# Layer 0 of a two-layer diffusion trunk: fewer gathered rows traced beside each expert product worked out ahead

## The chip, the cores and the metric

One Trainium2 chip, one of its cores. The metric is device time in microseconds (us) of one execution, lower is better. Times of different runs of the kernel before: 5150.38, 5170.73 and 5175.75 us, median 5170.73 us.

## The reference, cut to what matters

Two layers over 512 latent tokens and 256 context tokens, model width 1024. Each layer is a mixer and then PEER, an expert network with 128 x 128 = 16384 experts. For every token and each of 8 heads, 16 experts are retrieved, so 128 experts per token:

```python
    def block(xb):
        q = (xb @ w_q).reshape(P_TOKEN_BLOCK, P_HEADS, 2, P_DQ // 2)
        s = jnp.einsum('nhpd,hpkd->nhpk', q, keys).astype(jnp.float32)
        s_top, i_top = lax.top_k(s, P_TOPK)
        ...
        u = u_tab[idx]
        v = v_tab[idx]
        act = jax.nn.gelu(jnp.einsum('nd,nhkd->nhk', xb, u).astype(jnp.float32), approximate=False)
        return jnp.einsum('nhk,nhkd->nd', (gate * act).astype(v.dtype), v)
```

In layer 0 both streams need it: the 512 latent tokens and the 256 context tokens. The context result is read first by layer 1.

## The kernel before, in words

The kernel computes PEER in two ways. **Dense**, for the latent tokens of layer 0: all 16384 experts are multiplied with all 512 tokens, 128 experts (index j) at a time, and a gate table G that is zero for experts not chosen weighs the activations. **Sparse**, for the two tiles of 128 context tokens: `sparse` (L1710) gathers, one of 128 chosen experts after the other, a row of 1024 floats for each of the 128 tokens from the u table (indirect DMA issued by GpSimd, L1729), multiplies and sums it on VectorE (L1741); then the same from the v table, accumulated on VectorE (L1754). One such gather and its VectorE instruction is called a row here. Two tiles x 2 tables x 128 make 512 rows in layer 0.

The sparse work is a Python generator that yields after each row. `pull(n)` (L470) adds n to an account and takes one row out of the generator for each whole unit. Calls of `pull` stand at fixed places of the dense work, so they decide after which dense instruction a row is traced. `issue_after(s.anchor)` (L1728) holds each gather on GpSimd behind the last weight split (L354 or L233) that was traced before it. The row buffers `ga` are a ring: 4 in the first stage of layer 0 (`NS[0]`), 5 in the second (`NX` more), 7 in the second of layer 1. The tracing order is a priority: a planner (`schedule_with_timeline_sim`) lays out the order of each engine's instructions from it, and on the chip every engine keeps that order.

`peer(0)` (L1769) has two stages.

Stage one, the ahead stage. `retrieve` (L1567) makes 16 query products and scores, takes the top 16 on VectorE and decodes indices; `spread` (L1676) turns each tile's choice into one-hot matrices on VectorE and ScalarE (L1693, L1700, L1701, L1703), multiplies them on TensorE (L1705), collects 32 tokens in one staging buffer (`stg`, L1706) and writes it to the table G in DRAM. Between them, `u_step` (L1804) works out 96 of the 128 dense products activation(u_j . x) ahead of need (TensorE L250, L251, L253) and writes them to DRAM (AD). Query and u products both take 8 matmuls on each of those three lines. The generator of retrieve and spread yields a price; each 5.5 of it pays for a `u_step`, followed by a `pull`:

```python
                    if p == 0 and s.gens:
                        s.pull(2 * R0[l])
                    while price > UP[l] and n < spill:
                        price -= UP[l]
                        u_step()
                        n += 1
                        s.pull(R0[l])
                while n < spill:
                    u_step()
                    n += 1
                    s.pull(RT[l])
```

The yield with p == 0 comes 8 times (once per head). `UP[0]` is 5.5, `spill` 96, `RT[0]` 2. These lines are L1869 to L1879. The other prices: 3.6 per head for the top 16 of each of the three later token tiles (8 heads each), 2.6 four times per tile in the decoding of the indices, 1.2 thirty-two times per tile in `spread`; there are four tiles.

Stage two, the dense stage, `peer_out` (L1892). For each of 128 j: the activations (96 from AD, 32 worked out here) times G (L1932), split into high and low parts (ScalarE L230, GpSimd L233), the v rows likewise (L230, VectorE L233), then 18 matmuls into six accumulators (L1998 to L2000) and 6 more into a tile (L1916 to L1918) that VectorE adds to the result (L1920). A `pull(s.rate)` follows each j and each of the 32 products; `s.rate = s.left() / (128.0 + 128 - len(old)) + 0.02` (L1907) spreads what is left of the rows over these 160 places. `peer_out` starts only when all of G is written.

Layer 1 has the same two stages with other numbers (`R0[1]` = 1.6).

Of the kernel before, what the change touches and what calls it, by code (L numbers as in the profile page):

```python
# [27 lines left out]
GT = (0, 1)  # L28
HT = (0, 1)
PD = (1, 2)  # L30
R0 = (2.0, 1.6)
RG = (2, 1)
NR = 2
NV = 3
# [173 lines left out]
class Net:  # L208
# [1560 lines left out]
    def peer(s, l):  # L1769
# [11 lines left out]
        with ExitStack() as st:  # L1781
# [30 lines left out]
            with ExitStack() as es:  # L1812
# [53 lines left out]
                for p in s.chain([s.retrieve(l, ep, tp_, pk, (psq, 'q'), (psm, 'hs'), (hh, hl), tiles, max(ng + nh, 1),  # L1866
                                             done, after), halves()]):
                    price += p
# [8 lines that stand above are left out]
# [198 lines left out]
```

## Time and profile before

| | |
|---|---|
| median of 3 runs | 5170.73 us (5150.38 to 5175.75) |
| profiled execution, its own time | 5158.15 us |
| span of its trace | 5156.4 us |
| TensorE busy | 4427.5 us, 86% |
| VectorE busy | 3975.7 us, 77% |
| GpSimd busy | 2888.2 us, 56% |
| ScalarE busy | 2022.6 us, 39% |
| mean granted TensorE clock | 0.927 |

The profiled execution lies 12.58 us under the median of the runs and inside their spread. Busy shares are means over stages with different limits, so they are read stage by stage below. Windows are in us from the start of the span: in layer 0 the retrieval and the products ahead run from about 936 to 1872, the dense stage from 1872 to 2840; in layer 1 the dense stage runs from 4435 to 5122.

### The profile page before, as it was taken

How to read it: one execution, taken by the hardware profiler on the slowest of the kernel's cores; microseconds unless marked ns; L12 is line 12 of the kernel's file. 1: busy time of each engine (PE TensorE's matmuls, PEld its weight loads, DVE VectorE, ACT ScalarE, POOL GpSimd, SP SyncE). 2: the span in 40 equal slices, each digit the busy share in tenths (PEclk: the TensorE clock that was granted, in tenths of full speed). 3: DMA queues.
4: the chain of work that ended last, by engine and by line, in shares of the span. 5: the costliest groups of instructions: out<-in, count | busy, mean ns of one | idle time of the engine just before them, and what ended most of it. 6: DMA issues, size and time to landing. Idle time of an engine off the chain costs nothing. (4 is left out here: it accounts for less than half of the span.)

```text
span 5156.4 us, 74375 instructions
## 1 busy us (share of the span) xinstructions
PE 4427.5 (86%) x26350; PEld 3625.3 (70%) x26350; DVE 3975.7 (77%) x7777; ACT 2022.6 (39%) x3979; POOL 2888.2 (56%) x2244
## 2 busy tenths in 40 slices
PE   7899988788889979999999898897966677799897
PEld 5777667567778867777777675785765676677775
DVE  4665568899998868787878674662699989888896
ACT  3544442225555642222222365332333553233332
POOL 2342233776667846656665320542476686688884
PEclk8999998899999989999999997998988888899999
DMA  5432124677778988877787210004377787899995
GB/s 193 156 115 62 58 78 160 220 262 249 238 267 304 321 279 312 288 285 282 284 295 287 88 52 21 6 6 151 106 221 249 248 304 271 310 335 339 340 352 211
DMA packets 453558, 1109.55 MB, mean 215 GB/s; under 512 B 40640, under 2 KB 204864, under 8 KB 449088
## 3 DMA queue, kind: packets, MB, share of 16 engines
q1 hardware_dynamic: 323872, 633.91, 36.4%
q0 software_dynamic: 129312, 470.87, 25.5%
q8 instruction: 208, 3.41, 0.3%
q14 instruction: 166, 1.36, 0.1%
HBM read 995.58 MB, written 109.05 MB: 214 GB/s over the span
## 5 line engine op out<-in xcount | busy, mean ns | idle before, releaser
L354 POOL TENSOR_TENSOR wlo<-wraw,whi 128x512 fp32r<-128x512 f32 x810 | 1148.4, 1441 | 982.1 <-ACT whi L351 910.8
L1729 POOL DMA_INDIRECT ga<-in_pu,idx x512 | 672.5, 1313 | 361.8 <-DVE ga L1741 105.1
L253 PE MATMUL u<-hh,wlo 128*128 128x512 f32 (+1 forms) x2048 | 746.0, 365 | 103.1 <-POOL wlo L354 103.0
L1741 DVE SCALAR_TENSOR_TENSOR ga<-ga,htok 128x1024 f32<-128x1024 f32 x512 | 742.6, 1464 | 94.0 <-DMA ga<-in_pu,idx 93.6
L250 PE MATMUL u<-hh,whi 128*128 128x512 f32 (+1 forms) x2048 | 744.3, 363 | 51.7 <-DVE xl L1920 24.1
L251 PE MATMUL u<-hl,whi 128*128 128x512 f32 (+1 forms) x2048 | 734.6, 359 | 0.0
L351 ACT ACTIVATE whi<-wraw 128x1024 fp32r<-128x1024 f32 x405 | 426.2, 1054 | 748.4 <-PE u L251 361.0
L1754 DVE SCALAR_TENSOR_TENSOR sacc<-ga,sact,sacc 128x1024 f32<-128x1024 f32 x381 | 563.7, 1480 | 112.0 <-DMA ga<-in_pv,idx 107.4
L1729 POOL DMA_INDIRECT ga<-in_pv,idx x384 | 502.4, 1308 | 210.0 <-DVE sacc L1754 76.3
L253 PEld LDWEIGHTS u<-hh,wlo 128*128 128x128 f32 x2048 | 422.2, 206 | 154.2 <-POOL wlo L354 112.7
L250 PEld LDWEIGHTS u<-hh,whi 128*128 128x128 f32 x2048 | 423.5, 207 | 107.1 <-DVE xl L1920 33.4
L251 PEld LDWEIGHTS u<-hl,whi 128*128 128x128 f32 x2048 | 422.6, 206 | 40.9
L233 DVE TENSOR_TENSOR vl<-vraw,vh 128x768 fp32r<-128x768 f32 (+1 forms) x256 | 356.5, 1399 | 92.7 <-ACT vh L230 71.9
L1705 PE MATMUL g<-ohB,ohA 128*128 128x128 f32 x1792 | 300.4, 297 | 135.9 <-DVE ohB L1703 109.1
L1705 PEld LDWEIGHTS g<-ohB,ohA 128*128 128x128 f32 x1792 | 265.1, 204 | 182.6 <-DVE ohB L1703 100.9
L230 ACT ACTIVATE vh<-vraw 128x768 fp32r<-128x768 f32 (+1 forms) x256 | 240.0, 946 | 286.2 <-PE acc L1999 229.3
L1703 DVE TENSOR_SCALAR ohB<-c_all,pt 128x128 f32<-128x128 f32 x512 | 319.1, 648 | 40.4 <-PE g L1705 34.7
L2000 PE MATMUL acc<-wh,vl 128*128 128x512 f32 x768 | 302.8, 394 | 23.2 <-DVE vl L233 22.3
L1998 PE MATMUL acc<-wh,vh 128*128 128x512 f32 x768 | 290.0, 393 | 27.0 <-ACT wh L230 27.0
L1999 PE MATMUL acc<-wl,vh 128*128 128x512 f32 x768 | 301.1, 392 | 9.1 <-POOL wl L233 9.1
L2015 PE MATMUL acc<-vl,wh 128*128 128x512 f32 x768 | 258.3, 402 | 27.1 <-DVE vl L233 27.0
L2014 PE MATMUL acc<-vh,wh 128*128 128x512 f32 x768 | 222.1, 399 | 45.6 <-ACT vh L230 25.2
(514 smaller groups left out, 10063.8 us busy)
## 6 DMA issues: line engine op xcount, KB each, us to landing
wraw<-in_uT SPq DMA_DIRECT2D x256, 512.0 KB
vraw<-in_pv SPq DMA_DIRECT2D x256, 512.0 KB
G<-stg SPq DMA_DIRECT2D x28, 2048.0 KB
wraw<-in_ada_w SPq DMA_DIRECT2D x96, 512.0 KB
wraw<-in_ew SPq DMA_DIRECT2D x64, 512.0 KB
G<-G SPq DMA_DIRECT2D x32, 1024.0 KB
wraw<-in_pwq SPq DMA_DIRECT2D x48, 512.0 KB
AD<-act SPq DMA_DIRECT2D x96, 256.0 KB
```

Source lines behind the costliest of these rows:

```text
L233: i = (lo_eng or nc.vector).tensor_tensor(lo, x, hi.bitcast(F32), OP.subtract)
L250: nc.tensor.matmul(o, a, hh[:, k], start=(k == 0), stop=False)
L251: nc.tensor.matmul(o, a, hl[:, k], start=False, stop=False)
L253: nc.tensor.matmul(o, b, hh[:, k], start=False, stop=(k == nk - 1))
L351: nc.scalar.activation(hi[:, :, 0:m], r[:, :, 0:m], AF.Copy)
L354: i = nc.gpsimd.tensor_tensor(lo[:, p, 0:m], r[:, p, 0:m], hi[:, p, 0:m].bitcast(F32), OP.subtract)
L1703: nc.vector.tensor_scalar(B, C['iota'], pt[:, 1, c:c + 1], pt[:, 2, c:c + 1], op0=OP.is_equal, op1=OP.mult)
L1705: nc.tensor.matmul(ps[:, n], A[:, n], B, start=True, stop=True)
L1729: nc.gpsimd.indirect_dma_start(out=ga, out_offset=None, in_=tab, in_offset=bass.IndirectOffsetOnAxis(ap=idx[:, k:k + 1], axis=0))
L1741: nc.vector.scalar_tensor_tensor(ga, ga, 1.0, htok, op0=OP.mult, op1=OP.mult, accum_out=act[:, k:k + 1])
L1754: nc.vector.scalar_tensor_tensor(acc, ga, act[:, k:k + 1], acc, op0=OP.mult, op1=OP.add)
L2000: nc.tensor.matmul(acc[d], b, wh, start=False, stop=sp)
```

## The change

One constant. `R0[0]` goes from 2.0 to 1.2. It is read at two places, both shown above: `pull(2 * R0[l])` after each of the 8 heads of the retrieval, and `pull(R0[l])` after each product worked out ahead while the retrieval and the spreading are being traced. `RT`, the pull beside the products that are left after that, stays 2. Rows not pulled there remain in `s.left()`, and L1907 spreads them along the dense stage.

```diff
 PD = (1, 2)
-R0 = (2.0, 1.6)
+R0 = (1.2, 1.6)
 RG = (2, 1)
```

## Rows read from the trace of the kernel before

**Rows 1.** Windows, all engines: window, length, busy us (instructions) PE PEld DVE ACT POOL; clock, DMA share, GB/s
```profile
936.00:1100.00 164.00, 137.80 (x594) 109.62 (x595) 139.78 (x309) 47.98 (x106) 138.41 (x102) 0.90 0.79 260
1100.00:1485.00 385.00, 325.99 (x1510) 265.31 (x1509) 378.76 (x980) 182.14 (x363) 254.49 (x184) 0.93 0.75 253
1485.00:1600.00 115.00, 101.99 (x495) 84.17 (x494) 112.52 (x247) 62.49 (x133) 80.52 (x56) 0.94 0.77 259
1600.00:1830.00 230.00, 229.93 (x1205) 195.76 (x1205) 186.69 (x216) 142.93 (x313) 180.49 (x130) 1.00 0.90 315
1830.00:1872.00 42.00, 11.88 (x65) 10.24 (x63) 15.90 (x27) 18.96 (x45) 3.44 (x3) 0.64 0.65 226
1872.00:2840.00 968.00, 904.54 (x3789) 724.62 (x3790) 776.76 (x900) 264.54 (x441) 617.41 (x455) 0.97 0.82 292
4435.00:5122.00 687.00, 629.88 (x2957) 519.22 (x2958) 587.83 (x564) 224.92 (x312) 554.88 (x398) 0.97 0.93 334
```

**Rows 2.** Waits of PE, 1100 to 1600: total us, times, longest
```profile
PE g L1705 <- DVE ohB L1703: 46.1, 36, 3.6
```

**Rows 3.** Timeline of PE, 1830 to 1873: start us, us, instructions [idle before]
```profile
1839.51 5.67 PE L1705 MATMUL g<-ohB,ohA 128*128 128x128 f32 x26 [5.49 <-ACT stg L1706]
...
1872.29 1.22 PE L1998 MATMUL acc<-wh,vh 128*128 128x512 f32 x2 [22.14 <-ACT wh L230]
```

**Rows 4.** Waits of DVE, 1872 to 2840
```profile
DVE sacc L1754 <- DMA ga<-in_pv,idx: 67.3, 25, 6.5
DVE ga L1741 <- DMA ga<-in_pu,idx: 60.2, 27, 6.5
DVE ad L1932 <- DMA ad<-AD: 53.8, 26, 8.0
```

**Rows 5.** Waits of PE, 1872 to 2840
```profile
PE u L250 <- DVE xl L1920: 24.1, 18, 2.7
PE acc L2000 <- DVE vl L233: 22.3, 19, 3.1
```

**Rows 6.** Windows of L251 alone: PE busy (instructions), PEld, clock, DMA share, GB/s
```profile
1100.00:1485.00 385.00, 151.52 (x364) 72.86 (x364) 0.93 0.75 253
```

**Rows 7.** Windows of L1741 alone (u rows): DVE busy, two instructions a row
```profile
936.00:1100.00 164.00, 93.64 (x113) 0.90 0.79 260
1100.00:1485.00 385.00, 98.96 (x144) 0.93 0.75 253
1872.00:2840.00 968.00, 180.66 (x256) 0.97 0.82 292
4435.00:5122.00 687.00, 132.13 (x184) 0.97 0.93 334
```

**Rows 8.** Windows of L1754 alone (v rows): DVE busy, one instruction a row
```profile
1100.00:1485.00 385.00, 29.33 (x20) 0.93 0.75 253
1600.00:1830.00 230.00, 91.91 (x66) 1.00 0.90 315
1872.00:2840.00 968.00, 203.11 (x138) 0.97 0.82 292
4435.00:5122.00 687.00, 189.86 (x127) 0.97 0.93 334
```

**Rows 9.** Groups of POOL, 1872 to 2840: busy us, mean ns
```profile
L1729 POOL DMA_INDIRECT ga<-in_pv,idx x139 | 171.6, 1234 | 82.9 <-DVE sacc L1754 50.5 <-issue 17.5 <-DMA vraw<-in_pv 5.2
```

**Rows 10.** One line, L1703, 1100 to 1600: duration ns min/median/max
```profile
L1703 DVE TENSOR_SCALAR ohB<-c_all,pt x144: 318/336/3254, 1186.1 to 1598.0; 128x128 f32<-128x128 f32 x144
```

**Rows 11.** Timeline of POOL, then of DVE, around 1307
```profile
1305.01 2.51 POOL L1729 DMA_INDIRECT ga<-in_pu,idx  x1 [0.30 <-DVE ind L1642]
1307.54 2.52 POOL L354 TENSOR_TENSOR wlo<-wraw,whi 128x512 fp32r<-128x512 f32 x2
...
1306.91 3.23 DVE L1703 TENSOR_SCALAR ohB<-c_all,pt 128x128 f32<-128x128 f32 x1
```

**Rows 12.** Groups of DVE, 1100 to 1600: busy us, mean ns
```profile
L1703 DVE TENSOR_SCALAR ohB<-c_all,pt 128x128 f32<-128x128 f32 x144 | 83.7, 591 | 1.7 <-PE g L1705 1.6
```

## The prediction

> **What bounds the kernel now.** I read the windows of all engines first, then the windows of single lines for where the gathered rows lie, then the waits in the two stages of layer 0.
>
> The kernel has no single bound. From 1100 to 1485, in the ahead stage, VectorE is busy 378.76 of 385 us (98.4%) and TensorE 325.99 (84.7%) [rows 1]: VectorE is the limit, and 59 us of TensorE time are empty. The largest wait of TensorE there, 46.1 us in 36 times, is for a one-hot matrix from VectorE [rows 2]. [...] At the end of the stage, 1830 to 1872, TensorE works 11.88 of 42 us [rows 1]: the last spreading trails after the last product, and 22.14 us pass while G is stored and the first loads come [rows 3]. In the dense stage, 1872 to 2840, TensorE is busy 904.54 of 968 us (93.4%) and VectorE 776.76 (80.2%) [rows 1]. VectorE's idle time there is waits for transfers, 67.3 + 60.2 us for gathered rows and 53.8 us for stored activations [rows 4]; TensorE's waits for VectorE are 24.1 + 22.3 us [rows 5]. So rows are to leave a stretch where VectorE is the limit and enter one where TensorE is.
>
> **How many rows move.** The code's prices add up to 4 x 10.4 (decoding) + 3 x 28.8 (top 16) + 4 x 38.4 (spreading) = 281.6; at 5.5 a product that pays for 51 products. Rows pulled before: 8 x 4.0 = 32 at the heads and 51 x 2 = 102 beside the products. After: 8 x 2.4 = 19.2 and 51 x 1.2 = 61.2. So 12.8 + 40.8 = 53.6 rows move to the dense stage. That the trace follows the code can be seen: 364 instructions of L251 from 1100 to 1485 are 45.5 products [rows 6], which should bring 91 rows; 72 u rows and 20 v rows are there [rows 7, 8]. The dense stage holds 128 + 138 = 266 of the 512 rows now [rows 7, 8] and should hold about 320, 2.5 for each j in place of 2.1.
>
> **Price of a row.** Early, 93.64 us for 57 rows, 1.64 us each [rows 7]. In the bound stretch (98.96 + 29.33) / 92 = 1.39 us; in the dense stage (180.66 + 203.11) / 266 = 1.44 us [rows 7, 8]. VectorE loses 12.8 x 1.64 = 21 us before 1100 and 40.8 x 1.39 = 57 us in 1100 to 1485 or just behind, and gains 53.6 x 1.44 = 77 us in the dense stage. The gathers move with their rows, 53.6 x 1.23 = 66 us [rows 9]; GpSimd is busy 64% in the dense stage and 81% in layer 1's [rows 1].
>
> **The bound stretch, 1100 to 1485.** VectorE would need 379 - 57 = 322 us, less than the 326 of TensorE, which becomes the limit. Bounds: at best TensorE runs without a gap, 385 - 326 = 59 us gained; at worst nothing, if each gap has another cause that was hidden. Between them I interpolate over two stretches of the same stage [rows 1]: VectorE 97.8% goes with TensorE 88.7% (1485 to 1600), VectorE 81.2% with TensorE 100% (1600 to 1830), 0.68 points for each point. With the new ratio of work, 322 to 326, both are met at TensorE 93%: 326 / 0.93 = 351 us, so **-34 us**. What is late next is TensorE itself, and then the product's split on GpSimd and ScalarE.
>
> **The retrieval, 936 to 1100.** VectorE 85%, TensorE 84% [rows 1]: neither engine is full, so the 21 us of work lie partly under waits for something else. Bounds 0 and -21; **-6 us**, nearer to 0 since the scores and products of the retrieval, not the rows, give TensorE its work here.
>
> **The end of the stage.** The last spreading runs from 1830 to 1850, after the products, with TensorE nearly empty; its last big piece starts at 1839.51 [rows 3]. The spreading is late because VectorE was full; with 57 us taken from VectorE before it, it comes closer to the last product. Bounds 0 and -20 (the store and the first loads stay); **-8 us**. The ahead stage together: -34 - 6 - 8 = -48 us.
>
> **The dense stage.** 77 us of VectorE work and 66 us of gathers on GpSimd come in. If the stage kept its length, VectorE would be at (777 + 77) / 968 = 88%. Lower bound 0: there are 191 us of VectorE idle time. Upper bound: each row pays in full, its 1.44 us and the present wait per row, (67.3 + 60.2) / 266 = 0.48 us, together 103 us. The nearest row is layer 1's dense stage [rows 1, 7, 8]: 92 + 127 = 219 rows in 687 us, 31.9 in 100 us, and there VectorE is at 85.6%, GpSimd at 81%, the DMA share at 0.93, and TensorE still at 91.7%. The changed stage comes to 320 rows in some 986 us, 32.4 in 100 us. With TensorE at that 91.7%, 904.5 / 0.917 = 986 us: **+18 us**. Layer 1 has seven row buffers and this stage five, which is why I keep the upper bound. In bytes a row is 128 x 1024 x 4 = 0.52 MB, so 28 MB more on 292 GB/s x 968 us = 283 MB: 316 GB/s over 986 us, below the 334 of layer 1's dense stage.
>
> [...] At 1306.91 a one-hot of VectorE takes 3.23 us, where the median is 0.336, while a gather (to 1307.52) and a weight split (1307.54 to 1310.06) follow each other on GpSimd [rows 10, 11]. [...]
>
> **The sum.** -48 + 18 = -30 us on the profiled execution's 5158.15 us: 5128 us. That execution lies 12.6 us under the median of the runs, 5170.73, so on the median it is **5141 us**.
>
> **The rivals.**
> (a) The dense stage takes back what the ahead stage gives: each row costs it about half of the full 1.92 us, 51 us, net +3, 5174 us. For it: VectorE in the dense stage hardly ever waits for anything but transfers [rows 4], so it is close behind TensorE all the time. Against it: layer 1's dense stage.
> (b) The gather loop of the dense stage becomes the limit, slower. A gather can go out only when the row five places before it has been used, then must land, and VectorE, which keeps its order, holds the value splits and result adds behind it. VectorE's ledger is 777 us of work and 181 of waits in 968 us; if the waits don't shrink, 77 + 26 us are added in full: -48 + 103 = +55, 5226 us. It decides from the point where a row in the dense stage costs over (48 + 26) / 53.6 = 1.4 us. For it: 127.5 us of waits for rows already [rows 4], and five buffers. Against it: these waits came 25 and 27 times, about as often as the 32 products are worked out there, not at each of 266 rows, so the loop is not what runs all the time, and a VectorE that comes later finds its row landed.
> (c) The freed VectorE time isn't used: the spreading is held by its one staging buffer and by the planned order, the ahead stage gives only 8 us, and the sum is +10, 5181 us. For it: 5.49 us of wait for that buffer at the end [rows 3]. Against it: the 46.1 us of waits for one-hots [rows 2].
> (d) Both sides go well: -59 - 6 - 20 ahead and +5 dense, -80, 5091 us. For it: the gapless 1600 to 1830.
> That the change would not move the rows is ruled out by the agreement of 91 with 92.
>
> **How the numbers follow.** Forecast 0.48, (a) 0.17, (b) 0.17, (c) 0.08, (d) 0.10. What a measurement of this kernel can tell from no change is about 0.5%, 26 us. The forecast's own range is 5115 to 5165; three quarters of it lie beyond 26 us, so 0.36 faster and 0.12 the same. (a) counts as the same, (b) as slower, (d) as faster, (c) 0.05 same and 0.03 slower. Faster 0.46, the same 0.34, slower 0.20. The range leaves out the outer part of (b) and the edge of (d): 5090 to 5210 us.
>
> **What would show it.** In the changed profile: 72 + 20 rows beside those 45.5 products become about 55; TensorE over them from 85% to over 90%, and its wait for one-hots under half of 46.1 us; about 320 rows in the dense stage; that stage 985 us or so, VectorE at 86 to 88%, and its waits for gathered rows not above the present 127.5 us. It is wrong if the ahead stage (936 to 1872) is less than 30 us shorter, which speaks for (c), or if the dense stage is over 40 us longer, which speaks for (a) or (b): then TensorE's waits for VectorE there would be far above 46 us.

## The result: faster, by twice the forecast

The changed kernel takes 5101.47 us (median of four runs, 5089.76 to 5112.47), the kernel before 5165.32 beside it: ratio 0.9874, 95% interval 0.9854 to 0.9895. The profiled execution takes 5096.44 us, 62 less than that of before; 30 less was forecast. The time lies inside the outer range of 5090 to 5210 us and outside the forecast's own, 5115 to 5165; the direction is right, the size is not.

Windows of the changed kernel, all engines, columns as in [rows 1], with its own stage limits (the dense stage now begins at 1827 and not 1879):

```profile
936.00:1100.00 164.00, 143.65 (x627) 114.23 (x628) 124.40 (x305) 49.28 (x110) 125.61 (x93) 0.90 0.69 224
1100.00:1485.00 385.00, 341.98 (x1688) 280.98 (x1687) 370.04 (x1120) 207.95 (x426) 216.74 (x160) 0.98 0.64 223
1485.00:1600.00 115.00, 115.00 (x601) 98.00 (x601) 92.14 (x130) 72.71 (x160) 87.88 (x65) 1.00 0.88 317
1600.00:1780.00 180.00, 171.20 (x886) 144.74 (x885) 147.74 (x163) 106.88 (x231) 143.91 (x102) 0.99 0.90 321
1780.00:1827.00 47.00, 22.44 (x104) 18.09 (x103) 19.74 (x28) 19.26 (x41) 15.14 (x11) 0.74 0.69 227
1827.00:2732.00 905.00, 877.59 (x3784) 709.71 (x3783) 894.26 (x927) 263.37 (x436) 619.11 (x481) 0.99 0.94 327
4380.00:5062.00 682.00, 623.38 (x2963) 512.29 (x2962) 592.76 (x570) 224.78 (x310) 552.20 (x398) 0.99 0.94 336
```

The instruction counts of TensorE (the first number in brackets) tell how far its program has come. In the first three stretches the changed kernel does 2916 matmuls, before 594 + 1510 + 495 = 2599 [rows 1]. In the dense stage the work is the same and the length is not. One line gives that length, the second of the 18 matmuls of each j, first and last start; before, then changed:

```profile
L1999 PE MATMUL acc<-wl,vh x768: 387/389/793, 1878.7 to 2843.0; 128*128 128x512 f32 x192
```

```profile
L1999 PE MATMUL acc<-wl,vh x768: 387/389/632, 1826.8 to 2731.4; 128*128 128x512 f32 x192
```

The stage starts 51.9 us earlier and takes 904.6 us in place of 964.3, 59.7 less, although more rows lie in it. The rows of the changed kernel, L1741 (u, two instructions a row) and then L1754 (v, one), to hold against [rows 7, 8]:

```profile
936.00:1100.00 164.00, 67.09 (x87) 0.90 0.69 224
1100.00:1485.00 385.00, 83.16 (x123) 0.98 0.64 223
1827.00:2732.00 905.00, 200.91 (x256) 0.99 0.94 327
...
1827.00:2732.00 905.00, 279.92 (x166) 0.99 0.94 327
2732.00:2800.00 68.00, 33.15 (x26) 0.60 0.66 217
```

294 rows are in the stage and 26 behind its end, 320 together, as forecast. The 26 have a price. The waits of VectorE for transfers in the stage (for [rows 4]), and then TensorE behind the stage:

```profile
DVE ad L1932 <- DMA ad<-AD: 8.9, 5, 6.6
DVE sacc L1754 <- DMA ga<-in_pv,idx: 2.5, 1, 2.5
```

```profile
2737.63 1.09 PE L239 MATMUL o<-c_all,a 128*128 128x128 f32 x8 [2.90 <-DVE xl L1920]
2787.15 1.94 PE L239 MATMUL o<-c_all,a 128*128 128x128 f32 x8 [48.43 <-DMA a<-AC]
```

The waits for gathered rows fall from 127.5 to 2.5 us; and TensorE stands 48.4 us until the second tile's sum, whose last rows come late, has gone to DRAM (AC) and back. From the last L1999 to layer 1's first matmul of the same kind it is 1648.7 us, before 1592.7. Together: 51.9 + 59.7 - 56.0, and 4.1 in layer 1's dense stage, are 59.7 of the 62 us.

The 51.9 us say too little of the ahead stage. Up to the first query matmul of layer 0 TensorE, VectorE, ScalarE and GpSimd run the same instructions in the same order in both kernels (5513, 1659, 866 and 250 that count as busy), and the changed execution comes there 9.7 us later; before, then changed:

```profile
926.88 1.22 PE L250 MATMUL q<-hh,whi 128*128 128x512 f32 x2 [8.96 <-ACT hh L230]
```

```profile
936.60 1.22 PE L250 MATMUL q<-hh,whi 128*128 128x512 f32 x2 [9.37 <-ACT hh L230]
```

In the profiled executions of the twelve experiments below it starts between 929.0 and 941.0, so this is the spread of single executions and not the edit. From it to the first L1999 it is 951.8 us before and 890.2 changed: the ahead stage is 61.6 us shorter.

### The profile page after: what moved, and what is told of

The parts are those of the page before. It is cut to its first block, busy times and chain, and to the rows that moved or that the text cites. A ratio compares the mean times of both kernels' runs of the same rounds, so it can differ in the third digit from the quotient of the medians.

```text
span 5094.5 us, 74416 instructions
## 1 busy us (share of the span) xinstructions
PE 4379.3 (86%) x26350; PEld 3595.2 (71%) x26350; DVE 4044.1 (79%) x7777; ACT 2022.8 (40%) x3979; POOL 2841.9 (56%) x2244
## 5 line engine op out<-in xcount | busy, mean ns | idle before, releaser
L354 POOL TENSOR_TENSOR wlo<-wraw,whi 128x512 fp32r<-128x512 f32 x810 | 1108.7, 1392 | 1052.6 <-ACT whi L351 991.8
L253 PE MATMUL u<-hh,wlo 128*128 128x512 f32 (+1 forms) x2048 | 734.0, 359 | 112.5 <-POOL wlo L354 112.4
L1741 DVE SCALAR_TENSOR_TENSOR ga<-ga,htok 128x1024 f32<-128x1024 f32 x512 | 741.1, 1462 | 47.0 <-DMA ga<-in_pu,idx 46.7
L250 PE MATMUL u<-hh,whi 128*128 128x512 f32 (+1 forms) x2048 | 727.8, 356 | 22.8 <-ACT act L1889 18.4
L251 PE MATMUL u<-hl,whi 128*128 128x512 f32 (+1 forms) x2048 | 720.9, 352 | 0.0
L351 ACT ACTIVATE whi<-wraw 128x1024 fp32r<-128x1024 f32 x405 | 426.3, 1054 | 630.9 <-PE u L251 263.5
L1754 DVE SCALAR_TENSOR_TENSOR sacc<-ga,sact,sacc 128x1024 f32<-128x1024 f32 x381 | 597.1, 1567 | 48.9 <-DMA ga<-in_pv,idx 43.3
L233 DVE TENSOR_TENSOR vl<-vraw,vh 128x768 fp32r<-128x768 f32 (+1 forms) x256 | 368.2, 1444 | 92.1 <-ACT vh L230 91.9
L251 PEld LDWEIGHTS u<-hl,whi 128*128 128x128 f32 x2048 | 413.9, 202 | 37.4
L1703 DVE TENSOR_SCALAR ohB<-c_all,pt 128x128 f32<-128x128 f32 x512 | 314.4, 637 | 43.0 <-PE g L1705 42.4
L1999 PE MATMUL acc<-wl,vh 128*128 128x512 f32 x768 | 302.9, 394 | 9.4 <-POOL wl L233 9.1
```

Source lines behind the costliest of these rows:

```text
L233: i = (lo_eng or nc.vector).tensor_tensor(lo, x, hi.bitcast(F32), OP.subtract)
L250: nc.tensor.matmul(o, a, hh[:, k], start=(k == 0), stop=False)
L251: nc.tensor.matmul(o, a, hl[:, k], start=False, stop=False)
L253: nc.tensor.matmul(o, b, hh[:, k], start=False, stop=(k == nk - 1))
L351: nc.scalar.activation(hi[:, :, 0:m], r[:, :, 0:m], AF.Copy)
L354: i = nc.gpsimd.tensor_tensor(lo[:, p, 0:m], r[:, p, 0:m], hi[:, p, 0:m].bitcast(F32), OP.subtract)
```

## The experiments

The question was why a dense stage with more rows is shorter. Rivals at first: START (it begins 52 us earlier, against other neighbours), LOAD (more rows change the mix of work), RING (the loop of five row buffers is what ran before), and LAG (with the higher rate rows are asked for earlier than they are used). After four runs a fifth theory took the place of LAG, told behind them.

**The ahead stage's half alone.** The changed kernel without 54 v rows of the second tile, so that the dense stage has as few rows as before:

```diff
-                s.todo = 512
+                s.todo = 458
+        nv = 74 if l == 0 and q == 0 else 128
-        for k in range(128):
-            ga = take(s.I[f'pv{l}'], k)
+        for k in range(nv):
+            ga = take(s.I[f'pv{l}'], k, nv)
```

> The changed kernel (R0[0] = 1.2), but the last 54 v rows of the second context tile are left out, so the dense stage of layer 0 again gets about 262 rows. Theory LAG: the dense stage of the changed kernel is 60 us shorter because 2.5 rows for each j are more than the planned order can place, so every row's VectorE instruction falls further behind its gather and no longer waits for it to land; with 262 rows that is gone, so first to last L1999 matmul is 955 to 970 us as before (964), the waits of VectorE for gathered rows are 110 to 140 us, there is no 48 us wait for the context result at the end, and only the ahead stage's 52 us remain: ratio to before 0.989 to 0.991 (about 5113 us). Rival START: the dense stage is shorter because of what the ahead stage leaves it (order, early G): it stays at 900 to 915 us, waits under 20 us, no end wait, ratio about 0.978 (5053 us).

Measured: 5095.95 us, ratio 0.9851 (0.9819 to 0.9883). The stage starts at 1818.8 and takes 961.5 us, as long as before, with the old waits, and no wait of 48 us behind it:

```profile
DVE ad L1933 <- DMA ad<-AD: 66.0, 33, 6.6
DVE sacc L1755 <- DMA ga<-in_pv,idx: 54.2, 23, 5.7
DVE ga L1742 <- DMA ga<-in_pu,idx: 45.4, 24, 4.8
```

The early start alone shortens the stage by 3 us and not by 60: START falls. LAG's own numbers were met in part only: 99.6 us of waits for rows where 110 to 140 were named, and a ratio of 0.9851 where 0.989 to 0.991 was.

**The dense stage's half alone.** The kernel before, with 54 v rows of the second tile gathered a second time:

```diff
-                s.todo = 512
+                s.todo = 566
+        nv = 182 if l == 0 and q == 0 else 128
```

> The kernel before (R0[0] = 2.0), but the second context tile gathers 54 of its v rows a second time at the end, so the dense stage gets about 318 rows and the ahead stage is that of before. LAG: the dense stage, first to last L1999, is 900 to 915 us in spite of 54 rows more, VectorE's waits for rows under 10 us, a wait of 40 to 55 us for the context result at its end: net about -10 us, ratio 0.997 to 0.999. The prediction's step (TensorE at 91.7%, +18 us): dense 980 to 990 us, ratio 1.003 to 1.006. START: dense 980 us or more, since the ahead stage is the old one.

Measured: 5156.84 us, ratio 0.9973 (0.9959 to 0.9986). With 54 more rows asked for, of which 28 run inside the stage and 26 behind it, the stage takes 905.3 us, 59 less than before. Waits of VectorE in the stage, then of TensorE behind it:

```profile
DVE ad L1933 <- DMA ad<-AD: 9.7, 3, 6.2
DVE sacc L1755 <- DMA ga<-in_pv,idx: 1.3, 1, 1.3
DVE ga L1742 <- DMA ga<-in_pu,idx: 1.3, 2, 0.9
...
PE o L239 <- DMA a<-AC: 47.0, 1, 47.0
```

So both effects, the short stage and the wait behind it, come with the rows that were added to the dense stage, and the end wait takes most of the gain away.

**The same rows, asked for sooner.** The kernel before with the rate of layer 0's dense stage times 1.25:

```diff
-            s.rate = s.left() / (128.0 + 128 - len(old)) + 0.02
+            s.rate = (1.25 if l == 0 else 1.0) * s.left() / (128.0 + 128 - len(old)) + 0.02
```

> The kernel before, all 512 rows, R0[0] = 2.0; only s.rate of layer 0's dense stage is 1.25 times as high, so the same 262 rows are traced earlier along it than they can be placed, and are used up shortly before its end. LAG: it is the distance between gather and use that counts, not the number of rows: dense stage 900 to 915 us, VectorE's waits for rows under 10 us, no wait at the end, ratio 0.987 to 0.990 (about 5105 us). Rival LOAD (VectorE must be full to be rid of the stalls, or the number of rows matters): dense above 945 us, ratio above 0.996.

Measured: 5106.33 us, ratio 0.9872 (0.9841 to 0.9903). The stage takes 898.8 us, waits for rows 1.0 us, none behind the stage. No row is added, and the gain is there: LOAD falls. The price of a row stays open: the run before this one has 28 more rows in its stage and takes 6.5 us longer, 0.23 us a row, but against the run at 1.08 times below, which has the rows of this one and takes 882.6 us, the difference is 22.7 us, 0.8 us a row. The planned orders differ too, so neither is a price of rows alone.

**One more row buffer.** `NX = 1` to `NX = 2`:

> The kernel before with NX = 2: six row buffers in place of five in both dense stages' extra ring (eight in place of seven in layer 1). LAG: each row stays one j behind its gather in the planned order, so a further buffer changes nothing: dense stage of layer 0 950 to 970 us, waits for rows above 100 us, ratio 0.997 to 1.003. Rival RING (the loop of five buffers is what VectorE waits for): waits for rows fall below 60 us, dense 920 to 940 us, ratio 0.992 to 0.996.

Measured: 5183.34 us, ratio 1.0031 (1.0011 to 1.0051); the stage takes 979.4 us with these waits:

```profile
DVE ad L1932 <- DMA ad<-AD: 75.1, 29, 5.9
DVE sacc L1754 <- DMA ga<-in_pv,idx: 49.5, 24, 5.9
DVE ga L1741 <- DMA ga<-in_pu,idx: 45.4, 25, 5.2
```

RING falls, and with it the place at which rival (b) of the prediction put its loop. LAG had named 950 to 970 us and over 100 us of waits for rows (94.9 measured).

**What the traces then showed.** GpSimd of the kernel before, one cycle of four j and one product (columns: start, duration, instruction, idle time before it and what ended it), and what VectorE sees of it:

```profile
2246.57 1.28 POOL L233 TENSOR_TENSOR wl<-ad,wh 128x512 fp32r<-128x512 f32 x1
2250.09 0.95 POOL L1729 DMA_INDIRECT ga<-in_pu,idx  x1 [2.24 <-DVE ga L1741]
2252.57 1.15 POOL L1729 DMA_INDIRECT ga<-in_pu,idx  x1 [1.52 <-DVE ga L1741]
2259.14 2.99 POOL L354 TENSOR_TENSOR wlo<-wraw,whi 128x512 fp32r<-128x512 f32 x2 [5.43 <-ACT whi L351]
2264.64 1.46 POOL L233 TENSOR_TENSOR wl<-act,wh 128x512 fp32r<-128x512 f32 x1 [2.52 <-ACT wh L230]
2266.26 1.49 POOL L1729 DMA_INDIRECT ga<-in_pu,idx  x1 [0.15 <-issue]
...
2275.52 1.23 DVE L1741 SCALAR_TENSOR_TENSOR ga<-ga,htok 128x1024 f32<-128x1024 f32 x1 [5.74 <-DMA ga<-in_pu,idx]
```

Between the gathers at 2252.57 and 2266.26 none goes out for 13.7 us: GpSimd keeps its order, and the next in it is the split of the next u chunk (L354), which waits 5.43 us for ScalarE's half (L351), and that starts when the running product is done (ScalarE stood 12.09 us for TensorE's L251 there). VectorE uses up the five landed rows and then stands for 5.74 us. This comes about once for each of the 32 products; the 25 and 27 waits of [rows 4] follow each other, those of u rows in the first half of the stage and those of v rows in the second, one or two in each cycle. In the planned order of the kernel before, 2.1 gathers on average stand between the last weight split and the chunk's split; in the changed kernel, in the second and the third run 4.0 to 4.1. Hence the next theory, called HOLD or ORDER: the place of the gathers in GpSimd's planned order decides, not how many rows there are. The plans differ in more than this one place: in most cycles the kernel before has 6 or 7 gathers between the four weight splits and then the 2 ahead of the chunk's split, the next run 5 and then 4.

**A smaller rate.** The same edit as the early-rows run, with 1.08:

> The kernel before with one number changed: layer 0's dense stage asks for rows 1.08 times as fast (1.25 in the early-rows run). In the planned order four gathers then stand between the last weight split and each split of a u chunk on GpSimd (2.1 in the kernel before), while the rows run little further ahead of the plan than before. HOLD (the dense stage is short because gathers stand just ahead of GpSimd's held split, so that a split that waits for its buffer holds nobody up): the stage takes 895 to 920 us, waits of VectorE for gathered rows under 15 us, ratio 0.986 to 0.991. LAG (it is short because rows are asked for earlier, and the more so the larger the surplus): a third of the surplus gives a third of the gain, 940 to 955 us, ratio about 0.996, waits for rows about 80 us.

Measured: 5077.70 us, ratio 0.9830 (0.9812 to 0.9848); the stage takes 882.6 us, waits for rows 1.2 us. A third of the surplus brings more than the whole (and more than the 895 to 920 us that HOLD named): LAG falls. One cycle on GpSimd:

```profile
2255.84 1.30 POOL L233 TENSOR_TENSOR wl<-ad,wh 128x512 fp32r<-128x512 f32 x1
2258.85 1.69 POOL L1729 DMA_INDIRECT ga<-in_pu,idx  x1 [1.71 <-DVE ga L1741]
2260.85 1.43 POOL L1729 DMA_INDIRECT ga<-in_pu,idx  x1 [0.30 <-issue]
2262.59 0.94 POOL L1729 DMA_INDIRECT ga<-in_pu,idx  x1 [0.30 <-DVE vl L233]
2264.42 1.15 POOL L1729 DMA_INDIRECT ga<-in_pu,idx  x1 [0.90 <-PE u L253]
2265.59 3.16 POOL L354 TENSOR_TENSOR wlo<-wraw,whi 128x512 fp32r<-128x512 f32 x2
...
2271.74 1.75 POOL L1729 DMA_INDIRECT ga<-in_pu,idx  x1 [0.16 <-issue]
```

Four gathers fill the time in which the split of before waits; it waits for nothing now, and the stretch without a gather is 7.3 us.

**The split put later.** The kernel before, with the chunk's split behind the last weight split of the plan:

```diff
+            with (s.tc.issue_after(s.anchor) if s.free else ExitStack()):
                 for k in range(0, DT, DT // 2):
```

> The kernel before with the split of a u chunk on GpSimd (layer 0's dense stage alone) put behind the last weight split of the plan, so that it stands between weight splits and no longer with two gathers ahead of it and none behind; the number of rows asked for and their rate are as before. HOLD: the split then comes later, when its buffer is free, gathers are no longer held behind it, and the dense stage takes 900 to 930 us with waits for gathered rows under 50 us; ratio 0.987 to 0.993. LAG or a rival that needs more rows asked for early: nothing changes, 955 to 968 us, ratio about 1.0. Against both: a product that waits longer for its chunk's split would show as a wait of TensorE for POOL and make the stage longer.

Measured: 5172.22 us, ratio 1.0016 (1.0000 to 1.0031), the stage 977.6 us: the expectation of HOLD is missed. The chunk's split never waits, the waits for rows are halved, but GpSimd now stands at the weight split of the worked-out activation (260.4 us of such waits in the stage, 85.3 before), and VectorE waits for stored activations:

```profile
DVE ad L1935 <- DMA ad<-AD: 79.2, 27, 7.5
DVE ga L1743 <- DMA ga<-in_pu,idx: 32.8, 24, 3.8
DVE sacc L1756 <- DMA ga<-in_pv,idx: 30.4, 26, 3.4
```

The hold moved and did not go. That the chunk's split is the only place to mend is not so; what holds is the narrower statement on gathers ahead of it.

**1.04 and 1.06 times.** In the planned orders the rows' counts at each j hardly differ from those of 1.08, and the gathers ahead of the split do, 2.3 and 2.9 on average. In the traces, VectorE has used 381 and 450 rows before TensorE's 65th and 97th j in the kernel before, 384 and 458 at 1.04, 388 and 462 at 1.06, 388 and 464 at 1.08. So 1.04 stands between, and 1.06 is the clean test, with the counts of 1.08 and another order:

> The kernel before with rows asked for 1.04 times as fast in layer 0's dense stage. Its rows come hardly earlier or later than at 1.08 times (375 against 377 rows placed before the 64th j, 446 against 451 before the 96th), but the planned order of GpSimd still has only 2.3 gathers between the last weight split and the held split of a u chunk, as the kernel before has with 2.1, and not the 4.0 of 1.08 times. ORDER (where the gathers lie against the held split decides): the dense stage takes 950 to 965 us, waits for rows over 80 us, ratio 0.996 to 1.001. RATE (the faster rate by itself decides): most of what 1.08 times gave, 895 to 915 us, ratio 0.985 to 0.989.

> The same with 1.06 times: the planned order has 2.9 gathers ahead of the held split, some cycles with 2 and some with 4, while the rows' counts are those of 1.08 times (377 and 450). ORDER: between, 910 to 945 us, waits for rows 30 to 80 us, those waits in the cycles with 2 gathers ahead; ratio 0.988 to 0.996. RATE: the same as 1.08 times, 880 to 895 us, ratio 0.983 to 0.985.

Measured: 5160.93 us, ratio 0.9976 (0.9959 to 0.9993), the stage 956.2 us; and 5141.07 us, 0.9951 (0.9934 to 0.9968), the stage 933.0 us. Waits for rows at 1.04, then at 1.06:

```profile
DVE sacc L1754 <- DMA ga<-in_pv,idx: 58.3, 27, 7.4
DVE ga L1741 <- DMA ga<-in_pu,idx: 46.5, 19, 6.7
```

```profile
DVE sacc L1754 <- DMA ga<-in_pv,idx: 54.9, 22, 6.1
DVE ga L1741 <- DMA ga<-in_pu,idx: 27.0, 10, 5.2
```

ORDER is met twice, but for a little more of row waits at 1.06 (81.9 us, 30 to 80 expected) and RATE is not. The cycles of single executions, taken from the timelines of GpSimd and VectorE in the middle of the stage, say it without a comparison of whole kernels:

| kernel | gathers ahead | cycles | split waits, mean us | row waits in the cycle, mean us | cycle, mean us |
|---|---|---|---|---|---|
| before | 2 | 24 | 2.7 | 4.2 | 31.0 |
| 1.04 times | 2 | 17 | 1.9 | 4.4 | 31.7 |
| 1.06 times | 2 | 10 | 2.7 | 4.4 | 31.7 |
| 1.06 times | 3 | 12 | 0.1 | 2.5 | 29.2 |
| 1.06 times | 4 | 5 | 0.2 | 0.4 | 27.2 |
| 1.08 times | 4 | 24 | 0.1 | 0.0 | 27.9 |
| changed | 4 | 18 | 0.0 | 0.0 | 28.6 |

The cycle at 1.08 is 3.1 us shorter than before; over the 28 such cycles of the stage this is 87 us, near the 81.7 by which the stage is shorter. Cycles of one kernel at 1.06 times differ as the kernels do. The split's own wait is not all of it: with three gathers ahead it is 0.1 us, and rows still wait 2.5 us.

**A third buffer for the chunk's halves.**

```diff
-                tc.tile_pool(name=s.name("ad"), bufs=ND_) as ad, \
+                tc.tile_pool(name=s.name("ad"), bufs=ND_) as ad, s.more(0, 1 - l), \
```

> The kernel before with a third buffer for the two split halves of a u chunk in layer 0's dense stage; the planned order of GpSimd's gathers and splits is the same as before, rows and rate too. HOLD (the split of the chunk on GpSimd waits for its buffer and holds the gathers behind it): the 67.7 us of GpSimd's waits for that split fall under 15 us, VectorE's waits for rows fall from 127.5 to under 60 us, and the stage takes 905 to 935 us, ratio 0.987 to 0.994. If that hold only moves to GpSimd's next wait (the weight split), as when the split was put elsewhere: 950 to 970 us, ratio 0.998 to 1.002.

Measured: 5180.59 us, ratio 1.0031 (1.0017 to 1.0046), the stage 952.2 us. GpSimd's waits for the split and VectorE's for rows:

```profile
POOL wlo L354 <- ACT whi L351: 61.9, 20, 6.6
...
DVE sacc L1754 <- DMA ga<-in_pv,idx: 67.1, 24, 7.4
DVE ga L1741 <- DMA ga<-in_pu,idx: 55.4, 25, 5.6
```

Inconclusive: the wait that the buffer was to remove is still there, since the kernel splits one chunk further ahead with it and then waits for a buffer as before. What a stage with the order of before and no held split would take stays open. Nor is the whole kernel faster by the 12 us of its stage: from the last L1999 to layer 1's dense stage it takes 1613.0 us, 20 more than before.

So it is shown that the planned order, with the same rows, is worth up to 82 us of this stage, and that short cycles go with more gathers ahead of the chunk's split. That this one place is the cause is argued: neither of the two edits made at the split itself shortened the stage as the order did (977.6 and 952.2 us).

**Towards a better kernel.** 1.6 steps of gathering with each product ahead and the rate times 1.25; then 1.2 steps, the rate times 1.25 and `RT[0]` at 2.6:

> The kernel before with 1.6 steps of gathering with each product ahead (2 before, 1.2 in the changed kernel) and layer 0's dense stage asking for rows 1.25 times as fast. HOLD: the dense stage takes 900 to 915 us although some 25 more rows lie in it, no wait of TensorE for a stored row's load at its end, and the ahead stage gives half of its 52 us, so 5075 us, ratio 0.983. If the gains of the two stages don't add (the end wait of 48 us comes back): 5110 us, ratio 0.989.

> The kernel before with 1.2 steps of gathering with each product ahead, as in the changed kernel, layer 0's dense stage asking for rows 1.25 times as fast, and the cap on its rows raised from 2 to 2.6 for each j, so that the rows that the ahead stage leaves can all come inside the stage. HOLD: the ahead stage is 52 us shorter, the dense stage takes 900 to 920 us with some 320 rows, and no wait of 48 us for a stored row at its end: 5050 to 5065 us, ratio 0.979. If 2.6 rows for each j are more than VectorE can take (its busy time over 900 us), the dense stage comes to 930 to 950 us and the sum to about 5090 us, ratio 0.985.

Measured: 5073.62 us, ratio 0.9833 (0.9812 to 0.9854), the stage from 1848.9, 903.7 us, no wait behind it: both gains at once, as expected. And 5092.98 us, 0.9857 (0.9838 to 0.9876), the stage 898.2 us and 6.8 us of wait behind it, but starting at 1872.1 and not at 1827. That expectation has an error: `RT[0]` is no cap of the dense stage, it paces the rows beside the products left at the end of the ahead stage. The planned order of this kernel has 24 more rows ahead of the dense stage than the changed one (215 and 191), and the end of the ahead stage takes back the 45 us: that it is these rows is argued, not shown.

VectorE's order has another number: between the first and the last product with G (L1932) of layer 0's dense stage stand 285 rows in the changed kernel and in both of these, 286 in the next, whether the rate is times 1, 1.25 or 1.08. The changed kernel has 320 to place, so 35 come behind the last L1932, and 26 of them behind TensorE's last L1999.

> Three edits to the kernel before together: 1.6 steps of gathering with each product ahead, rows 1.08 times as fast in layer 0's dense stage, and the third buffer of the chunk's halves there. If the third buffer adds to the order's gain: 5045 to 5065 us, ratio 0.978. If the hold was the whole cause and the order has already taken it: the same as without the buffer, 5070 to 5080 us, ratio 0.983.

Measured for the last kernel (1.6 steps, rate times 1.08, the third buffer): 5056.35 us, ratio 0.9790 (0.9769 to 0.9812), the best of all, 45 us under the changed kernel. The number is the expected one, the place is not: its stage takes 898.1 us (903.7 with 1.6 steps and 1.25), and 16 of the 17 us between the two lie from the stage's end to layer 1's dense stage (1583.4 and 1599.5 us). It changed two things against that kernel, so which of them it is stays open.

## Why the prediction was wrong, step by step

- **Rows that move:** right. 61 are left in 1100 to 1485 beside 49 products, where 92 stood beside 45.5; 320 come to the dense stage or behind it.
- **The ahead stage, -48:** -51.9 by the start of the dense stage, -61.6 from the first query matmul on. By the number of a matmul in TensorE's order, the changed execution is 9.7 us late there, 4.0 us early at what came at 1100 before, 37.2 at 1485, 58.3 at 1600 and 51.9 at the first L1999. So the bound stretch gave 33 us (34 forecast) and the retrieval 14 (6 forecast, bound 21). The 21 us from 1485 to 1600 were not foreseen, and the rest up to the dense stage, at -8, lost 6 us: the store and the first loads stayed (22.14 us before, 22.55 after). TensorE came to 88.8% in the bound stretch and its wait for one-hots ([rows 2]) to 28.0 us, a little short of the 90% and the half that were named. The mean one-hot went from 591 ns [rows 12] to 555, some 5 us over 144 of them; what makes single ones as long as that of [rows 11], no run isolates. Rival (c) is refuted.
- **The dense stage, +18: the step that failed, and in its sign.** It was -59.7. The working took TensorE's share from layer 1's dense stage, 91.7%, as a price of dense rows; here it came to 97.0% with VectorE at 98.8%. The runs show that the 127.5 us of waits [rows 4] were no price of rows but went with the planned order: with the rows of before and a rate of 1.08 they are 1.2 us and the stage 882.6. Beside that stage the changed one is 22 us longer with 28 more rows, so +18 may not have been far off as a price of rows, which no run isolates; the 964.3 us that it was added to did not stay. A row's instructions on VectorE also came to 1.64 us where the prediction took over 1.44. The prediction had seen that the waits come about as often as the products worked out, used this against rival (b), and did not ask what stands on GpSimd at that moment. Its lower bound, nothing, should have been below nothing: a stall that follows from an order can go when an edit changes the order.
- **What stands behind the stage:** not looked at; 56.0 us were lost, since VectorE's order has 285 rows inside the stage and 320 were there. This nearly cancels the 59.7 us gained; that the time falls inside the outer range at all is owed to two misses of opposite sign, and is luck.
- **The rivals:** (a) and (b) are refuted by the second and fourth run. (d), both sides well, named 5091 us with a chance of 0.10; it came nearest to the 5101.47 us measured, by terms of other sizes: +5 in the dense stage, and nothing behind it.
- **"The waits for rows not above 127.5"** held, at 2.5, for a cause that was not in the prediction.

## What to carry to other kernels

An edit of how much work goes where also lays out every engine's order anew, and here that was worth as much as the edit: in the kernel before, 4% more of a pacing rate gave 7 us, 8% gave 87. Where waits come with a regular period, find what stands on the issuing engine once in each period, and what is queued behind it, before calling them a price of the work. And count what a stage has left when it ends: 26 of 320 rows took back nearly all that the stage had gained.

## What had not been expected of the hardware

Two pauses of TensorE cost it twice: the time in which it stands, and then 3.4 us at a granted clock of 0.50. In the kernel before, stretches of 8 us around them, in which it waits for VectorE's result add (L1920) and value split (L233), 2.68 us in the first and 1.44 + 0.95 us in the second, where the wait begins before 2248 (columns as in [rows 1]):

```profile
2208.00:2216.00 8.00, 8.00 (x36) 6.32 (x35) 6.12 (x9) 3.03 (x6) 6.79 (x6) 1.00 1.03 407
2216.00:2224.00 8.00, 5.32 (x17) 3.93 (x16) 6.01 (x9) 0.00 (x0) 3.58 (x3) 0.79 0.90 325
2224.00:2232.00 8.00, 8.00 (x37) 6.59 (x36) 7.02 (x12) 2.70 (x4) 3.55 (x2) 1.00 0.42 142
...
2248.00:2256.00 8.00, 6.32 (x20) 4.75 (x21) 8.00 (x14) 0.00 (x0) 2.10 (x2) 0.79 0.92 322
```

In the stretches in which TensorE stands for 1.7 to 2.7 us, the mean granted clock of the stretch is 0.79: in windows of half a microsecond it is 1.00 through the pauses, 0.50 from 2220.5 to 2223.5 and from 2251.0 to 2254.0, and then 1.00 again. 17 or 20 matmuls are done in place of 36 or 37: 0.31 us each and not 0.22. From the first to the last L1999 TensorE stands 27 times for over 1 us, and the clock is at 0.50 in 14 stretches, 54.6 us together; in the changed kernel it is 9 times and 3 stretches, 10.2 us. In that stage TensorE's busy time falls from 901.13 us for 3782 matmuls to 877.19 for 3783, with the granted clock going from 0.97 to 0.99. So 24 of the 59.7 us gained are busy time, and the idle time is the other 36; the forecast, which divided the busy time of before by a share, could not have found them.
